# Attention and gated-delta stage of a hybrid trunk: a scaling removed, and 52 PSUM copies moved from VectorE to ScalarE

## The chip, the core and the metric

The kernel runs on one core of a Trainium2 chip. The metric is device time in microseconds (us), median of several executions. Engines are named as in the profile: PE (TensorE), DVE (VectorE), ACT (ScalarE), POOL (GpSimd), and SP, whose queue starts most DMAs.

## The reference, cut to what matters

One step of a two-layer trunk over 128 context and 512 latent tokens, width 1024. The first layer runs two mixers beside each other on one input projection:

```
s = einsum('bqhgd,bkhd->bhgqk', q_blk, k) * hd ** -0.5        # hd = 64, so the factor is 1/8
p = softmax(s, axis=-1)
out = einsum('bhgqk,bkhd->bqhgd', p, v)                       # 8 query heads, 2 key heads
...
def step(s, inp):                                             # gated delta rule, 4 heads, 2 directions
    v_new = u_c - w_c @ s
    o_c = qd_c @ s + qk_c @ v_new
    s = s * dec_c + kd_c^T v_new
```

An output projection, an MLP, then a Mamba-2 (SSD) layer with its own MLP follow. Softmax gives the same numbers if the scores are computed as s' = -s, and exp(min(s') - s') stands for exp(s - max(s)).

## The kernel before, in words

Matrix products are float32, often as high and low halves. `even` runs the first layer; the part that matters here begins when the input projections end (229 us in the profiled execution) and ends when the output projection's first product, `rps` on line 328, starts (507.95 us). In it two strands share all engines:

- `attention`, a generator, runs 4 blocks (2 key heads by 2 pairs of query heads). A block turns its queries (`stacks`: `qtps`, copied by ACT into `qs`, line 1238), then for each of 4 latent query tiles and 2 heads does `scores` into `scps` (line 1243: 4 matmuls, 512 and 256 keys) and `softmax`: a maximum over 768 keys on DVE (line 1249, `amx`), a scaling of it by -1/8 on DVE (line 1250), the exponential on ACT with that as bias (line 1252), a reciprocal on DVE (line 1253), a scaling on ACT (line 1255). The weights `p` are turned on PE four blocks at a time (`ptps`, line 1294) and copied out of PSUM into `pp` and `ppr` (line 1297), by DVE and ACT in turn. At a block's end 12 products `avps` (line 1303) make the output. There is one buffer of `scps`, so the next scores wait for the exponential.
- `delta_head` runs once for each of 4 heads, on two sets of buffers, so that heads go in pairs. It inverts a triangular matrix (products on lines 1032 and 1038 with DVE work between), then scans 4 chunks in both directions. One step of the scan makes `v_new` in a PSUM bank `pv` (lines 1094, 1095), scales it into `vk` on DVE (line 1098), copies it into `vn` on DVE (line 1100), multiplies `vk` into the other columns of the same bank (line 1102), from which DVE makes the next state `s` (line 1104); `vn` goes into the output `ops` (line 1107). The context chunk has its own copies of these lines (1120, 1122, 1124, 1130). A head ends with a norm and five turns (line 1146).

The code's order is one head, nine pieces of attention, then the other heads. The list that each engine gets is made at build time by a scheduler that plays the program in simulated time, and which may move an instruction ahead of independent ones. So a change of an operation's engine also changes the order around it, the order in later stages included. Each engine then runs its own list strictly in order.

The weights of the output projection (`wraw`, line 264) land in the two buffers that attention uses for `pp` (`ring`), so their load waits for the last `avps` that reads them. The residual `x` (2.5 MB, line 788) is loaded into the space of the delta heads' buffers, from ACT's queue.

Of the kernel before, what the change touches and what calls it, by code (L numbers as in the profile page):

```python
# [14 lines left out]
AF = mybir.ActivationFunctionType  # L15
ALU = mybir.AluOpType
AX = mybir.AxisListType
# [3 lines left out]
P = 128  # L21
# [181 lines left out]
class Prog:  # L203
# [713 lines left out]
    def delta_head(self, dn, pd, h, st_, gt):  # L917
        nc, v, g = self.nc, self.nc.vector, self.nc.gpsimd
# [5 lines left out]
        quad = lambda ap: ap.rearrange("p (a b) -> p a b", b=P)  # L924
# [9 lines left out]
        for ts_, ids in lots:  # L934
            pt = bank()
# [153 lines left out]
        for n in range(4):  # L1089
            for d in range(2):  # L1090
                c = n if d == 0 else 3 - n
                t = c + 1
                pv = bank()
                nc.tensor.matmul(pv[:, 0:P], X[:, 1 - d, t, :], values(d, t), start=True, stop=False)
                nc.tensor.matmul(pv[:, 0:P], wn[d][:, t, :], st[d], start=False, stop=True)
                if n < 3:
                    vk = dn.tile([P, P], F32, name="vk", tag=f"vk{d}")
                    v.tensor_scalar(out=vk, in0=pv[:, 0:P], scalar1=gt["ek"][:, d, t, h:h + 1], scalar2=None, op0=ALU.mult)
                vn = dn.tile([P, P], F32, name="vn", tag=f"vn{d}", bufs=2)
                v.tensor_copy(vn, pv[:, 0:P])  # L1100
                if n < 3:
                    nc.tensor.matmul(pv[:, P:2 * P], kk[:, t, :], vk, start=True, stop=True)
                    s = dn.tile([P, P], F32, name="s", tag=f"s{d}", bufs=2)
                    v.scalar_tensor_tensor(out=s, in0=st[d], scalar=dec[d][:, c:c + 1], in1=pv[:, P:2 * P], op0=ALU.mult, op1=ALU.add)
                po = self.pout.tile([P, 512], F32, name="ops", tag="o")
                nc.tensor.matmul(po[:, 0:P], qd[d][:, c, :], st[d], start=True, stop=False)
                nc.tensor.matmul(po[:, 0:P], qk[d][:, t, :], vn, start=False, stop=True)
                if n < 3:
                    st[d] = s
                if n < 2:  # L1110
                    nc.scalar.activation(out=o[:, t, :], in_=po[:, 0:P], func=AF.Copy, scale=rq[:, t:t + 1])
                else:
                    v.scalar_tensor_tensor(out=o[:, t, :], in0=po[:, 0:P], scalar=rq[:, t:t + 1], in1=o[:, t, :], op0=ALU.mult, op1=ALU.add)

        vns = []
        for d in range(2):
            pv = bank()
            nc.tensor.matmul(pv[:, 0:P], X[:, 1 - d, 0, :], values(d, 0), start=True, stop=True)
            vk = dn.tile([P, P], F32, name="vk", tag=f"vk{d}")
            v.tensor_scalar(out=vk, in0=pv[:, 0:P], scalar1=gt["ek"][:, d, 0, h:h + 1], scalar2=None, op0=ALU.mult)  # L1120
            vn = dn.tile([P, P], F32, name="vn0", tag=f"vn{d}", bufs=2)
            v.tensor_copy(vn, pv[:, 0:P])
            vns.append(vn)
            nc.tensor.matmul(pv[:, P:2 * P], kk[:, 0, :], vk, start=True, stop=True)
            s = dn.tile([P, P], F32, name="s0", tag=f"s{d}", bufs=2)
            nc.scalar.copy(out=s, in_=pv[:, P:2 * P])
            nc.sync.dma_start(out=self.io["o_sd"][d, h], in_=s)
# [14 lines left out]
        for ts_, c, cu in (((0,), CTX_P, CTX_U), ((1, 2, 3, 4), LAT_P, LAT_U)):  # L1142
            pt = bank()
# [67 lines left out]
    def attention(self, at, psc, pacc, qkv, keys, ota):  # L1211
# [10 lines left out]
        def stacks(kv, pr):  # L1222

            c0 = 272 + kv * 256 + pr * 128
            x = qkv[:, :, c0:c0 + 128].rearrange("p t (h e) -> p t h e", e=64)
            qs = at.tile([P, 2, NTOK], F32R, name="qs", tag="qs", bufs=2)
            for ts_ in ((0, 1), (2, 3), (4,)):
                n = len(ts_)
                y = x[:, ts_[0]:ts_[0] + n]
                hl = at.tile([P, 768], F32, name="p", tag="p", bufs=3)[:, :n * 256].bitcast(F32R).rearrange("p (t h a b) -> p t h a b", h=2, a=2, b=64)  # L1230
                nc.scalar.copy(out=hl[:, :, :, 0], in_=y)
                v.tensor_tensor(out=hl[:, :, :, 1], in0=y, in1=hl[:, :, :, 0].bitcast(F32), op=ALU.subtract)
                hf = hl.bitcast(F32).rearrange("p t h a b -> p t h (a b)")
                pt = bank("qtps")
                for j, t in enumerate(ts_):
                    for i in range(2):
                        nc.tensor.transpose(pt[:, (i * n + j) * P:(i * n + j + 1) * P], hf[:, j, i], self.ident)
                nc.scalar.copy(out=qs[:, :, ts_[0] * P:(ts_[0] + n) * P], in_=pt[:, :2 * n * P].rearrange("p (i c) -> p i c", i=2))
            return qs

        def scores(out, qs, kv, i, t, k0, k1):
# [3 lines left out]
        def softmax(sc, p):  # L1245

            n = sc.shape[1]
            mx, sm = (at.tile([P, 2], F32, name=m, tag=m, bufs=3)[:, :n] for m in ("amx", "asm"))
            v.tensor_reduce(out=mx, in_=sc, axis=AX.X, op=ALU.max)
            v.tensor_scalar(out=mx, in0=mx, scalar1=-scale, scalar2=None, op0=ALU.mult)  # L1250
            for i in range(n):
                nc.scalar.activation(out=p[:, i], in_=sc[:, i], func=AF.Exp, scale=scale, bias=mx[:, i:i + 1], accum_out=sm[:, i:i + 1])
            v.reciprocal(out=sm, in_=sm)
            for i in range(n):
                nc.scalar.activation(out=p[:, i], in_=p[:, i], func=AF.Copy, scale=sm[:, i:i + 1])
# [5 lines left out]
        for kv in range(2):  # L1261
            for pr in range(2):
                o = ota[kv * 2 + pr]
                qs = stacks(kv, pr)
                yield

                sc = psc.tile([P, 2 * 512], F32, name="scps", tag="sc")
                for i in range(2):
                    scores(sc[:, i * P:(i + 1) * P], qs, kv, i, 0, 0, P)
                pc = at.tile([P, 2, P], F32, name="pc", tag="pc")  # L1270
                softmax(quad(sc[:, :2 * P]), pc)
                yield
                pt = bank("ptps")
                for i in range(2):
                    nc.tensor.transpose(pt[:, i * P:(i + 1) * P], pc[:, i], self.ident)
                pct = at.tile([P, 2, P], F32, name="pct", tag="pct")
                v.tensor_copy(pct, quad(pt[:, :2 * P]))
                yield

                for t in range(1, NT):  # L1280
                    cols = slice((t - 1) * P, t * P)
                    ps = []
                    for i in range(2):
                        sc = psc.tile([P, 2 * 512], F32, name="scps", tag="sc")
                        scores(sc[:, 0:512], qs, kv, i, t, P, P + 512)
                        scores(sc[:, 512:768], qs, kv, i, t, P + 512, P + 768)
                        ps.append(at.tile([P, 768], F32, name="p", tag="p", bufs=3))
                        softmax(sc[:, :768].rearrange("p (o k) -> p o k", o=1), ps[i].rearrange("p (o k) -> p o k", o=1))
                        yield
                    for j in range(3):  # L1290
                        pt = bank("ptps")
                        for n in range(4):
                            x = ps[j][:, n * P:(n + 1) * P] if j < 2 else ps[n // 2][:, (4 + n % 2) * P:(5 + n % 2) * P]
                            nc.tensor.transpose(pt[:, n * P:(n + 1) * P], x, self.ident)  # L1294
                        dst = ring[j][:, :, cols] if j < 2 else rest.rearrange("p i c q -> p (i c) q")[:, :, cols]
                        turn += 1
                        (v.tensor_copy if turn % 2 else nc.scalar.copy)(out=dst, in_=quad(pt))
                    yield
                acc = bank("avps")
                for c in range(6):  # L1300
                    for i in range(2):
                        x = ring[i][:, c] if c < 4 else rest[:, i, c - 4]
                        nc.tensor.matmul(acc[rows[i]], val(1 + c, kv), x, start=c == 0, stop=c == 5)  # L1303
                nc.scalar.copy(out=o[:, LAT_U], in_=acc)
                acc = bank("avps")
                for i in range(2):
                    nc.tensor.matmul(acc[rows[i], :P], val(0, kv), pct[:, i], start=True, stop=True)
                v.tensor_copy(o[:, CTX_U], acc[:, :P])
                yield
# [435 lines left out]
```

## Time and profile before

| | us |
|---|---|
| median of 3 runs (2148.13 to 2157.08) | 2155.83 |
| the profiled execution, device time | 2143.07 |
| its span, first to last instruction | 2141.2 |
| PE busy in the span | 2029.4 |
| DVE busy | 1376.8 |
| ACT busy | 935.4 |

The profiled execution took 1.87 us more than its span, and 12.76 us less than the median of the runs. A busy PE is a PE with matmuls in it, not one at its peak: the same four score matmuls count 0.95 us at the full granted clock and 1.65 us at half of it.

### The profile page before, as it was taken

How to read it: one execution, taken by the hardware profiler on the slowest of the kernel's cores; microseconds unless marked ns; L12 is line 12 of the kernel's file. 1: busy time of each engine (PE TensorE's matmuls, PEld its weight loads, DVE VectorE, ACT ScalarE, POOL GpSimd, SP SyncE). 2: the span in 40 equal slices, each digit the busy share in tenths (PEclk: the TensorE clock that was granted, in tenths of full speed). 3: DMA queues.
4: the chain of work that ended last, by engine and by line, in shares of the span. 5: the costliest groups of instructions: out<-in, count | busy, mean ns of one | idle time of the engine just before them, and what ended most of it. 6: DMA issues, size and time to landing. Idle time of an engine off the chain costs nothing.

```text
span 2141.2 us, 32845 instructions
## 1 busy us (share of the span) xinstructions
PE 2029.4 (95%) x13227; PEld 1827.7 (85%) x13227; DVE 1376.8 (64%) x2628; ACT 935.4 (44%) x1959; POOL 147.3 (7%) x106
## 2 busy tenths in 40 slices
PE   6999698898899999999899999999999899999998
PEld 4989686775797989898799999999888888989896
DVE  6386777874886767664678886787634634343445
ACT  4344457573342423233259866666531332323131
POOL 1031302100000000000000001111110000000000
PEclk9999789898999999999999999999999999999999
DMA  7261101005255343332234343333341221212121
GB/s 328 85 241 40 38 1 35 1 12 198 100 188 190 134 148 136 141 124 95 89 101 148 129 146 120 114 133 126 117 159 67 91 97 60 79 60 99 59 79 50
DMA packets 55834, 233.31 MB, mean 109 GB/s; under 512 B 6074, under 2 KB 21186, under 8 KB 33922
## 3 DMA queue, kind: packets, MB, share of 16 engines
q1 hardware_dynamic: 45952, 216.63, 28.4%
q10 hardware_dynamic: 9730, 14.58, 1.9%
q8 instruction: 104, 1.70, 0.3%
q14 instruction: 48, 0.39, 0.1%
HBM read 222.76 MB, written 8.43 MB: 108 GB/s over the span
## 4 chain that ended last, share of the span: by engine, by line
PE 85%; DVE 9%; DMA 2%; ACT 2%; issue 1%; POOL 0%; ACTq 0%; SPq 0%; DVEq 0%; POOLq 0%
PE gps L300 41%; PE rps L328 28%; PE yps L1648 2%; PE atps L750 2%; PE offps L1662 1%; PE scps L1243 1%; PE dps L1032 1%; DMA X<-growd 1%; PE stps L1679 1%; DMA wraw<-wall 1%; PE avps L1303 1%; PE dps L1038 1%; PE ptps L1294 1%; DVE wlo L275 1%; PE xkps L1498 1%
## 5 line engine op out<-in xcount | busy, mean ns | idle before, releaser
L300 PE MATMUL gps<-hh,whi 128*128 128x322 f32 (+3 forms) x1552 | 488.6, 316 | 1.4 <-ACT hh L412 1.4
L300 PE MATMUL gps<-hh,wlo 128*128 128x322 f32 (+3 forms) x1552 | 486.5, 314 | 0.0
L300 PE MATMUL gps<-hl,whi 128*128 128x322 f32 (+3 forms) x1552 | 485.6, 313 | 0.0
L300 PEld LDWEIGHTS gps<-hh,whi 128*128 128x128 f32 (+1 forms) x1552 | 292.3, 189 | 7.9 <-issue 5.1
L300 PEld LDWEIGHTS gps<-hl,whi 128*128 128x128 f32 (+1 forms) x1552 | 292.4, 188 | 3.2 <-issue 2.8
L300 PEld LDWEIGHTS gps<-hh,wlo 128*128 128x128 f32 (+1 forms) x1552 | 292.4, 188 | 2.1 <-issue 1.7
L328 PE MATMUL rps<-wlo,hidh 128*128 128x512 f32 x640 | 253.3, 396 | 0.0
L328 PE MATMUL rps<-whi,hidh 128*128 128x512 f32 x640 | 252.3, 396 | 0.0
L328 PE MATMUL rps<-whi,hidl 128*128 128x512 f32 x640 | 250.5, 395 | 0.0
L272 ACT CAST whi<-wraw 128x1024 fp32r<-128x1024 f32 (+2 forms) x132 | 140.3, 1065 | 247.1 <-PE rps L328 176.3
L284 DVE TENSOR_TENSOR wlo<-wraw,whi 128x1024 fp32r<-128x1024 f32 x88 | 107.4, 1225 | 191.5 <-ACT whi L283 191.5
L300 PE MATMUL gps<-yh,whi 128*128 128x320 f32 x1024 | 227.1, 311 | 0.2 <-ACT yh L412 0.2
L275 DVE TENSOR_TENSOR wlo<-wraw,whi 128x1024 fp32r<-128x1024 f32 (+3 forms) x123 | 157.8, 1283 | 100.7 <-ACT whi L272 100.3
L283 ACT CAST whi<-wraw 128x1024 fp32r<-128x1024 f32 x88 | 91.8, 1049 | 269.6 <-PE rps L328 188.5
L300 PEld LDWEIGHTS gps<-yh,whi 128*128 128x128 f32 x1024 | 172.6, 189 | 1.0 <-ACT yh L412 0.7
L300 PE MATMUL gps<-yh,wlo 128*128 128x320 f32 x512 | 158.6, 310 | 0.0
L328 PEld LDWEIGHTS rps<-whi,hidh 128*128 128x128 f32 x640 | 120.3, 188 | 29.3 <-issue 1.2
L328 PEld LDWEIGHTS rps<-wlo,hidh 128*128 128x128 f32 x640 | 120.3, 188 | 28.8 <-issue 0.6
L328 PEld LDWEIGHTS rps<-whi,hidl 128*128 128x128 f32 x640 | 120.3, 188 | 28.6
L485 DVE SCALAR_TENSOR_TENSOR macc<-wraw,condst,macc 128x512 f32<-128x512 f32 x196 | 137.2, 752 | 5.6 <-ACT macc L488 5.6
L650 DVE TENSOR_SCALAR hr<-gps 128x320 f32<-128x320 f32 x128 | 62.9, 492 | 105.7 <-PE gps L300 105.6
L651 ACT ACTIVATE hr<-hr 128x320 f32<-128x320 f32 x128 | 60.2, 470 | 150.8 <-DVE hr L650 149.3
(412 smaller groups left out, 3509.7 us busy)
## 6 DMA issues: line engine op xcount, KB each, us to landing
wraw<-wall SPq DMA_DIRECT2D x158, 1024.0 KB
bc<-afs SPq DMA_DIRECT2D x40, 512.0 KB
Q<-afr SPq DMA_DIRECT2D x64, 128.0 KB
xt<-xt ACTq DMA_DIRECT2D x1, 2560.0 KB
X<-growd SPq DMA_DIRECT2D x8, 320.0 KB
x<-x ACTq DMA_DIRECT2D x1, 2560.0 KB
xd<-x ACTq DMA_DIRECT2D x1, 2560.0 KB
x<-xd SPq DMA_DIRECT2D x1, 2560.0 KB
```

The costliest lines, as they stand in the source:

```text
L272: self.nc.scalar.copy(out=hi, in_=raw[:, :, c:c + m])
L275: eng.tensor_tensor(out=lo, in0=raw[:, :, c:c + m], in1=hi.bitcast(F32), op=ALU.subtract)
L283: self.nc.scalar.copy(out=hi, in_=x)
L284: self.nc.vector.tensor_tensor(out=lo, in0=x, in1=hi.bitcast(F32), op=ALU.subtract)
L300: self.nc.tensor.matmul(ps, ws[k // KT][q // 2][:, k % KT, :], xs[q % 2][k][:, c], start=k == 0 and q == 0, stop=k == n - 1 and q == 2)
L328: nc.tensor.matmul(ps, parts[x][k][:, c], w[y][:, j, :], start=k == 0 and q == 0, stop=k == n - 1 and q == 2)
L485: nc.vector.scalar_tensor_tensor(out=a, in0=x, scalar=w, in1=a, op0=ALU.mult, op1=ALU.add)
L650: nc.vector.tensor_scalar(out=r, in0=ps, scalar1=0.0, scalar2=None, op0=ALU.max)
L651: nc.scalar.activation(out=r, in_=r, func=AF.Square)
L750: nc.tensor.matmul(ps[:, :n], x[k][:, TOFF[t]:TOFF[t] + P], w[:, k, :], start=k == 0 and q == 0, stop=k == KT - 1 and q == 2)
L1032: nc.tensor.matmul(py[:, t * 32:(t + 1) * 32], m32[:, t, :], mixed(Xc, t, l), start=True, stop=True)
L1648: nc.tensor.matmul(py[q * 64:q * 64 + 64, pr * P:(pr + 1) * P], X[t](1 + d)[:, hh * 64:hh * 64 + 64], D[t][:, d, hh, :], start=d == 0, sto ...
```

## The change

Four edits. (1) The queries' halves leave PSUM multiplied by -1/8 (on ACT, where they were copied before), so the scores come out negated and scaled; the softmax takes their minimum, which is the exponential's bias as it is, and the DVE scaling on line 1250 (36 of them) is gone. (2) The copy `vn` in the scan is made by ACT (32 instructions). (3) So is `vn` of the context chunk (8). (4) Of the 48 copies of turned weights ACT now makes 36 and DVE 12, where it was 24 and 24.

```
                 vn = dn.tile([P, P], F32, name="vn", tag=f"vn{d}", bufs=2)
-                v.tensor_copy(vn, pv[:, 0:P])
+                nc.scalar.copy(out=vn, in_=pv[:, 0:P])
...
             vn = dn.tile([P, P], F32, name="vn0", tag=f"vn{d}", bufs=2)
-            v.tensor_copy(vn, pv[:, 0:P])
+            nc.scalar.copy(out=vn, in_=pv[:, 0:P])
...
-                nc.scalar.copy(out=qs[:, :, ts_[0] * P:(ts_[0] + n) * P], in_=pt[:, :2 * n * P].rearrange("p (i c) -> p i c", i=2))
+                nc.scalar.activation(out=qs[:, :, ts_[0] * P:(ts_[0] + n) * P], func=AF.Copy, scale=-scale, in_=pt[:, :2 * n * P].rearrange("p (i c) -> p i c", i=2))
...
-            v.tensor_reduce(out=mx, in_=sc, axis=AX.X, op=ALU.max)
-            v.tensor_scalar(out=mx, in0=mx, scalar1=-scale, scalar2=None, op0=ALU.mult)
+            v.tensor_reduce(out=mx, in_=sc, axis=AX.X, op=ALU.min)
             for i in range(n):
-                nc.scalar.activation(out=p[:, i], in_=sc[:, i], func=AF.Exp, scale=scale, bias=mx[:, i:i + 1], accum_out=sm[:, i:i + 1])
+                nc.scalar.activation(out=p[:, i], in_=sc[:, i], func=AF.Exp, scale=-1.0, bias=mx[:, i:i + 1], accum_out=sm[:, i:i + 1])
...
-                        (v.tensor_copy if turn % 2 else nc.scalar.copy)(out=dst, in_=quad(pt))
+                        (nc.scalar.copy if turn % 4 else v.tensor_copy)(out=dst, in_=quad(pt))
```

From line 1250 on, line numbers of the changed kernel are lower by one. PE's list at the end of the stage, before: the last scores, the last turns, the last head's five turns, attention's output products, then the output projection.

```order
L1106 MATMUL ops<-s,qd_4983 128x128
L1107 MATMUL ops<-vn,dt 128x128
L1146 MATMUL dps<-con,M 128x128 x5
...
L1294 MATMUL ptps<-con,p 128x128 x4
L1146 MATMUL dps<-con,M 128x128 x5
L1294 MATMUL ptps<-con,p 128x128 x8
L1303 MATMUL avps<-pp,qkv 64x512 x8
L1303 MATMUL avps<-ppr,vc 64x512 x4
L1307 MATMUL avps<-pct,qkv 64x128 x2
L328 MATMUL rps<-whi,op 128x512 x5
```

And now, from the last turns on:

```order
L1293 MATMUL ptps<-con,p 128x128 x4
L1106 MATMUL ops<-s,qd_4947 128x128
L1107 MATMUL ops<-vn,dt 128x128
L1118 MATMUL dps<-vb,X 128x128 x2
L1302 MATMUL avps<-pp,qkv 64x512 x8
L1302 MATMUL avps<-ppr,vc 64x512 x4
L1106 MATMUL ops<-s,qd_4946 128x128
L1107 MATMUL ops<-vn,de 128x128
...
L1130 MATMUL dps<-vn_5239,de 128x128
L1130 MATMUL dps<-vn_5251,dt 128x128
L328 MATMUL rps<-whi,op 128x512 x5
```

Before, all products of the scan (lines 1094 to 1130) stood ahead of the last two score groups; now attention's output products stand among the last products of the scan, and one head's five turns have gone behind the first 64 products of the output projection.

PE's list in the first pair's scan, with what each waits for (the name of an engine stands for its semaphore), before:

```order
L1102 MATMUL dps<-vk,dk_957 128x128 [waits DVE_49]
L1107 MATMUL ops<-vn,de 128x128 [waits Pool_49]
L1102 MATMUL dps<-vk,dk_957 128x128 [waits DVE_49]
L1094 MATMUL dps<-vb,X 128x128 [waits DVE_49,Activation_49]
L1095 MATMUL dps<-s,Xt 128x128
```

and now:

```order
L1102 MATMUL dps<-vk,dk_957 128x128 [waits Activation_49]
L1107 MATMUL ops<-vn,de 128x128 [waits Pool_49]
L1102 MATMUL dps<-vk,dk_957 128x128 [waits Activation_49]
L1094 MATMUL dps<-vb,X 128x128 [waits DVE_49]
L1095 MATMUL dps<-s,Xt 128x128
```

The state's product on line 1102, which reads `vk`, waited for DVE; it now waits for ACT, which makes `vn` out of the same bank.

ACT's list at that place, now:

```order
L1251 ACTIVATE p,asm<-scps,amx 128x768 [waits DVE_49]
L1296 COPY pp<-ptps 128x4x128 [waits PE_49]
L1000 ACTIVATE vb<-dv_958,beta 128x128 [waits PE_49] x2
L1100 COPY vn<-dps 128x128 [waits DVE_49] x2
L1254 ACTIVATE p<-p,asm 128x768 [waits DVE_49]
L1296 COPY ppr<-ptps 128x4x128 [waits PE_49]
L1251 ACTIVATE p,asm<-scps,amx 128x768 [waits DVE_49]
L1111 ACTIVATE M<-ops,rq_960 128x128 [waits PE_49]
L1000 ACTIVATE vb<-dv_958,beta 128x128 [waits PE_49,Activation_49] x2
L1100 COPY vn<-dps 128x128 [waits DVE_49] x2
```

The two `vn` of a step (one for each direction) have come in between the exponential and the scaling of a softmax, and wait for DVE's `vk`.

ACT's list at the end of the stage, now:

```order
L1122 COPY vn_5251<-dps 128x128 [waits DVE_49,Activation_49]
L1303 COPY ota_979<-avps 128x512 [waits PE_49]
L1126 COPY s_5242<-dps 128x128 [waits DMAHW7_49,PE_49]
L1126 COPY s_5254<-dps 128x128 [waits DMAHW0_49,PE_49]
L788 DMA x<-x 128x5120 [waits DMAHW3_49,DMAHW4_49,DMAHW2_49,PE_49]
L283 CAST whi<-wraw 128x1024 [waits DMAHW5_49]
```

The load of `x` stood well ahead of attention's last exponentials; it now stands behind the last attention output, right ahead of the first split of the output projection's weights.

## Rows read from the trace of the kernel before

**Rows 1.** The page: engines over the span.
```profile
PE 2029.4 (95%) x13227; PEld 1827.7 (85%) x13227; DVE 1376.8 (64%) x2628; ACT 935.4 (44%) x1959; POOL 147.3 (7%) x106
```
**Rows 2.** Windows: from:to, length, busy PE PEld DVE ACT POOL, clock, DMA.
```profile
234.00:258.00 24.00, 13.35 (x61) 11.22 (x62) 23.43 (x56) 13.19 (x40) 12.91 (x10) 0.64 0.12 33
314.00:341.00 27.00, 26.42 (x232) 24.69 (x231) 20.94 (x73) 20.88 (x53) 0.00 (x0) 1.00 0.06 16
362.00:386.00 24.00, 16.41 (x93) 10.68 (x93) 22.24 (x46) 12.42 (x35) 16.79 (x12) 0.90 0.06 16
420.00:479.20 59.20, 55.55 (x470) 48.41 (x469) 44.93 (x158) 44.16 (x114) 0.00 (x0) 1.00 0.02 6
479.20:508.00 28.80, 17.52 (x72) 9.48 (x69) 13.01 (x40) 12.93 (x29) 0.00 (x0) 0.75 0.49 182
500.00:2141.00 1641.00, 1596.64 (x9734) 1439.02 (x9730) 1031.05 (x1725) 675.42 (x1306) 60.88 (x41) 0.99 0.33 115
```
**Rows 3.** Chain that ended last, the stage's end: start, length, what.
```profile
490.54 0.99 ACT p L1252 x2
...
496.26 5.79 PE avps L1303 x16
502.06 4.77 DMA wraw<-wall
...
506.85 1.05 ACT whi L283
...
507.95 7.15 PE rps L328 x24
```
**Rows 4.** PE in order of time, 366 to 508 us: start, length, instructions, idle before.
```profile
367.38 3.66 PE L1303 MATMUL avps<-pp,qkv 128*64 128x512 f32 x16
370.87 1.88 PE L1303 MATMUL avps<-ppr,vc 128*64 128x512 f32 x8
...
477.82 0.94 PE L1243 MATMUL scps<-kst,qs 128*128 128x512 f32 x4
...
478.82 0.39 PE L1107 MATMUL ops<-vn,dt 128*128 128x128 f32 x2
...
479.59 0.60 PE L1294 MATMUL ptps<-con,p 128*128 128x128 f32 x4
...
496.26 5.76 PE L1303 MATMUL avps<-pp,qkv 128*64 128x512 f32 x16 [0.68 <-ACT ppr L1297]
```
**Rows 5.** Lines, 229 to 500 us: shapes, count, busy us, mean ns, idle before.
```profile
L1297 DVE COPY pp<-ptps 128x512 f32<-128x512 f32 x16 | 11.0, 687 | 1.2 <-PE ptps L1294 0.9
L1297 ACT COPY pp<-ptps 128x512 f32<-128x512 f32 x16 | 9.3, 582 | 11.0 <-PE ptps L1294 11.0
L1250 DVE TENSOR_SCALAR amx<-amx 128x1 f32<-128x1 f32 (+1 forms) x36 | 6.2, 173 | 0.3
```
**Rows 6.** Tile views: ns min/median/max of one, and waiters.
```profile
L1100 DVE COPY vn<-dps x32: 276/282/292, 314.7 to 473.7; 128x128 f32<-128x128 f32 x32
L1126 ACT COPY s<-dps x8: 247/262/276, 338.3 to 477.6; 128x128 f32<-128x128 f32 x8
L1255 ACT ACTIVATE p<-p,asm x32: 929/938/954, 242.9 to 492.0; 128x768 f32<-128x768 f32 x32
```
**Rows 7.** Waits, 229 to 500 us: us in total, times, longest.
```profile
ACT p L1252 <- DVE amx L1250: 13.8, 12, 3.7
PE scps L1243 <- ACT p L1252: 8.7, 7, 2.9
PEld dps L1102 <- DVE vn L1100: 1.4, 3, 0.6
```
**Rows 8.** DVE in order of time, around 245 us.
```profile
244.37 0.95 DVE L1249 TENSOR_REDUCE amx<-scps 128x1 f32<-128x768 f32 x1
...
246.64 0.15 DVE L1250 TENSOR_SCALAR amx<-amx 128x1 f32<-128x1 f32 x1
```
**Rows 9.** Windows while `x` lands.
```profile
482.00:486.00 4.00, 2.29 (x8) 1.65 (x8) 2.91 (x11) 2.79 (x8) 0.00 (x0) 0.69 0.96 410
```

## The prediction

> **What bounds the kernel now.** The page says PE is busy for 95% of the span and DVE for 64% [rows 1], so over the whole kernel nothing is to be had from DVE. The change touches one stage, from 229 us to the start of the output projection at 507.95 us, so I read that stage by windows [rows 2]; the reader should see three kinds of stretch. While a pair of heads scans (314 to 341, 420 to 479.2), PE is busy for 26.42 of 27 us and 55.55 of 59.2, at a granted clock of 1.00: PE is the bound there, DVE has a quarter of its time free. While a pair is prepared (234 to 258, 362 to 386), DVE is busy for 23.43 and 22.24 of 24 us, PE for 13.35 and 16.41, at a clock of 0.64 and 0.90: DVE is the bound. At the end (479.2 to 508) no engine is: PE 17.52 of 28.8 at a clock of 0.75, DVE 13.01, ACT 12.93.
>
> The end I read in the chain and on PE's own timeline. PE's last product of the scan starts at 478.82 us and takes 0.39 [rows 4]. What follows is attention alone, one engine after another: scores, DVE's maximum, ACT's exponential, turns, copies, the output products, and then 4.77 us for the first weights of the output projection, which land in attention's buffers, and 1.05 us for their split [rows 3]. So the stage ends with attention's strand, late by what that strand lost earlier. Where it lost time the waits tell: ACT waited 13.8 us for the scaling on line 1250, PE 8.7 us for the exponential [rows 7]. That scaling is short (0.173 us on the mean [rows 5]) but queues behind other DVE work: one maximum ends at 245.32 us and its scaling starts at 246.64 [rows 8].
>
> **The change, part by part.** All sums are against the profiled execution: 2143.07 us, a span of 2141.2 and 1.87 around it. The median of the runs, 2155.83, lies 12.76 higher; I take a difference worked out on the one for the other.
>
> DVE loses 36 scalings, 6.2 us; 40 `vn` copies of 0.282 us [rows 6], 11.3 us; and 12 copies of turned weights of 0.687 [rows 5], 8.2 us: 25.7 us in all. ACT gains 40 copies of 0.262 us (the row of line 1126 is the same shape from the same PSUM tiles [rows 6]), 10.5 us, and 12 of 0.582 [rows 5], 7.0 us: 17.5 us. The factor -1/8 rides on a copy that ACT made anyway, the minimum replaces a maximum of the same shape: both nothing, either way.
>
> *The end of the stage.* Attention's strand gets shorter by the wait for the scaling, and the built order has moved accordingly: its output products stand among the last products of the scan. So the 28.7 us between the end of the scan (479.21) and the first output product (507.95) go. What PE did in them must still be done, ahead of the scan's end, at full clock: six groups of turns at 0.60, two score groups at 0.94, and 24 output products at 3.66 + 1.88 [rows 4], 11.0 us. And the weights' load and split stay: 5.9 us from the last `avps` that reads the buffer (502.02) to the first product. PE's list has 1.88 us of `avps` and eight scan products, at 0.39 at most 3.1 us, in that time; about 1 us stays open. Term: -28.7 + 11.0 + 1 = **-16.7 us**. The head's five turns that went behind the first 64 products hide there: at the 7.15 us for 24 of the chain's last row [rows 3], 64 take 19 us, and the head's norm is needed only for products behind them.
>
> *The stretches where DVE is the bound.* No `vn` falls there. Of the scalings and weight copies (14.4 us over 279 us of stage) a share of 48/279 would be 2.5 us. Bounds: 0, and 5 if PE's lower clock comes back with it. I take **-2**.
>
> *`vn` on ACT.* 24 state products on line 1102 and 8 on line 1124 now wait for ACT, whose list holds exponentials and scalings of 0.94 us [rows 6]. Queued behind a stalled state product is PE's whole list, and then DVE's `s`. Below, this costs nothing: before, the same products waited for the copy on DVE, 1.4 us in three waits by the weight loads [rows 7]. Above, all 32 wait for a full 0.94: 30 us. ACT is busy 75% of the long scan stretch (44.16 of 59.2); half a length at that share is 0.35 us, 11 us over 32, if nothing lay between `vk` and its product on PE's list. There the scheduler has put turns or scores mostly. I take a quarter: **+3**.
>
> On the row, the product that writes the other half of the bank waited for a copy that it does not read (line 1102 for `vn`, 1.4 us [rows 7]). The Trainium skill has a rule for this: "PSUM — Partial Sum Buffer", section "PSUM bank collisions raise a hardware error", says that two engines may not touch one bank of the same partitions at once, two reads included, and are to be guarded by bank. By it `vk` on DVE and `vn` on ACT cannot lie beside each other, and moving the copy to a second engine shortens no step of the scan; the waits in the built order agree. A sum that let ACT copy while DVE scales would be lower by 32 copies of 0.28, 9 us; I don't take it.
>
> *The load of `x`.* It landed during the end of the stage at 410 GB/s [rows 9], with nothing waiting. Now its 2560 KB (2.62 million bytes) start beside the weights' load, on which PE waits. Bounds: 0, since the weights are asked for first, and 6.4 us (all of it at 410). I take **+1.5**.
>
> *Later stages.* The order in the SSD layer moved too, with no operation changed. PE is busy there for 1596.64 of 1641 us [rows 2]; I take nothing, and 3 us either way.
>
> Sum: -16.7 - 2 + 3 + 1.5 = -14.2. The profiled execution would take 2129, the median **2142 us**.
>
> **The rivals.** (a) *The scan hangs on ACT.* Each state product finds ACT inside an exponential or a scaling. With a mean wait w in place of my 0.09 us the sum is -17.2 + 32w: even at w = 0.54, slower by 0.5% at 0.87, and at 0.94 it is +13, 2169 us. For it: PE's list is strict, and the two `vn` of a step stand right behind an exponential. Against: PE's products between, and that the old wait was 1.4 us in all. (b) *The end changes its owner.* Attention is used up earlier, so the last steps of the scan lie bare: behind the last scores PE's list has three steps of one head, each at least three products of 0.39, a copy on ACT of 0.26 and two DVE operations like `vn` of 0.28, about 2 us plus hand-overs, with little to put between. Two of them bare and the same once more at the pair's end are 8 to 10 us; the sum is -5, 2151 us. For it: before, attention's products filled PE in the scan. Against: four groups of turns and the output products still stand among these steps. (c) *More is won.* With attention pulled ahead into the stretches where PE ran at 0.64 and 0.90, the clock there is 1.00: 13.35 us times 0.36 and 16.41 times 0.10 are 6.4 us; with the full 5 for DVE the sum is near -24, 2132 us. Against: POOL and the loads of `X` hold these stretches too.
>
> **How the numbers follow.** A measurement of this kernel tells a difference of about 0.5%, 10.8 us, from none. Chances: my forecast 0.45 (2136 to 2150), (b) 0.27, (a) 0.14, (c) 0.14. Faster by over 0.5% is below 2145: most of mine, all of (c), little of (b): 0.53. Slower is above 2166.6: most of (a): 0.12. The rest is 0.35. The range takes in (c), with the SSD layer's 3 us and the unknown load, and reaches into (a): 2122 to 2163, with some 0.15 left out, mostly above.
>
> **What would show it.** The changed profile should show the first output product 12 to 20 us earlier (near 492), attention's `avps` at full clock beside the scan's last products, no idle of several us on PE just ahead of them, DVE's busy time lower by about 26 us and ACT's higher by about 17. Waits of PE's line 1102 for ACT's `vn` of more than 10 us in all would show (a); PE idle between scan products after the last scores, (b); an unchanged clock in the preparation of both pairs speaks against (c); the first weights landing later than 4.77 us shows the load of `x`. I am wrong if the stage's end stays where it is, or if the time moves behind it.

## The result, and the profile after

The changed kernel took 2128.03 us (median of 6 executions, 2126.35 to 2136.43) against 2154.57 for the kernel before (6 executions, 2148.13 to 2157.08): a ratio on record of 0.9896, 95% interval 0.9872 to 0.9921 (it is not the quotient of the two medians, 0.9877). Both kernels run again gave 2130.05 and 2149.5, 0.9904 (0.9872 to 0.9936). So 19 to 27 us were won by the medians, 21 to 22 by the ratios. I had forecast 2142, from 2122 to 2163, with a chance of 0.53 for faster; the time lies in that range, but below the 2136 to 2150 of my own sum.

The page of the changed kernel, engines over the span, answers [rows 1]. DVE's busy time fell by 22.4 us, ACT's rose by 7.1. The 52 copies that ACT took over have 18.2 us by their lines, about what I had summed; the page's busy time rises less, since ACT's instructions overlap (its lines add up to over 1030 us in a busy time of 942.5):

```profile
span 2134.3 us, 32795 instructions
...
PE 2032.8 (95%) x13227; PEld 1835.8 (86%) x13227; DVE 1354.4 (63%) x2540; ACT 942.5 (44%) x2011; POOL 141.8 (7%) x106
```

The windows of the changed kernel, in the columns of [rows 2], with 262 to 300 us beside them; 479.20 to 500.00 ends at the new end of the stage:

```profile
234.00:258.00 24.00, 15.12 (x76) 12.87 (x76) 22.61 (x52) 15.81 (x44) 12.52 (x10) 0.78 0.12 34
262.00:300.00 38.00, 34.19 (x173) 29.40 (x174) 24.02 (x50) 17.18 (x35) 7.71 (x6) 0.65 0.00 1
...
362.00:386.00 24.00, 19.12 (x134) 17.84 (x134) 18.62 (x56) 16.31 (x47) 9.04 (x8) 0.86 0.13 39
420.00:479.20 59.20, 57.56 (x451) 51.45 (x452) 35.83 (x104) 37.60 (x98) 0.00 (x0) 0.90 0.01 2
479.20:500.00 20.80, 18.27 (x124) 12.88 (x122) 11.45 (x42) 12.85 (x42) 0.00 (x0) 1.00 0.24 88
500.00:2134.00 1634.00, 1592.47 (x9719) 1438.35 (x9719) 1034.26 (x1746) 674.43 (x1317) 55.76 (x41) 0.99 0.33 116
```

In both preparations PE does more than before and DVE less. The end is no longer half empty: PE is busy for 18.27 of 20.8 us at a clock of 1.00, where it was 17.52 of 28.8 at 0.75. In the long scan stretch, though, the clock is 0.90 where it was 1.00 (0.92 and 0.97 in the second profiles of the two kernels), and from 262 to 300 us it is 0.65 in both profiles of the changed kernel, where the kernel before has 0.78 and 0.86.

The chain that ended last, at the stage's end (start, length, what), answers [rows 3]:

```profile
490.48 3.59 PE avps L1302 x16
...
494.13 4.67 DMA wraw<-wall
...
498.82 1.05 ACT whi L283
...
499.92 15.16 PE rps L328 x64
```

PE in order of time at the same place (start, length, instructions, idle before and its releaser), for [rows 4]:

```profile
479.99 0.95 PE L1243 MATMUL scps<-kst,qs 128*128 128x512 f32 x4
...
490.41 3.65 PE L1302 MATMUL avps<-pp,qkv 128*64 128x512 f32 x16
...
498.49 0.39 PE L1130 MATMUL dps<-vn,dt 128*128 128x128 f32 x2
499.92 1.43 PE L328 MATMUL rps<-whi,op 128*128 128x512 f32 x5 [1.05 <-ACT whi L283]
```

The reader is to see that the two strands now end together. `avps` runs at full clock (3.65 us), the scan's last product ends at 498.88, behind it, and the output projection begins 1.04 us later, where there were 28.7 us between them. But the scan ends 19.7 us later than before (479.21, now 498.88), and so the first output product came only 8.0 us earlier. The second pair of profiles has the scan's end at 480.89 and 495.60 and the first output product at 509.66 and 496.73, 12.9 us apart.

The waits in the stage (us in total, times, longest), for [rows 7]:

```profile
PEld scps L1243 <- ACT p L1251: 7.6, 6, 2.3
...
PE scps L1243 <- ACT p L1251: 6.4, 6, 2.0
...
ACT p L1251 <- DVE amx L1249: 5.3, 7, 1.7
DVE s L1104 <- PE dps L1102: 3.8, 3, 2.3
...
PEld dps L1102 <- ACT vn L1100: 0.5, 2, 0.3
```

ACT's wait for the bias fell from 13.8 us to 5.3. PE's state product waits for ACT's `vn` no longer than it did for DVE's (0.5 us, 1.4 before). DVE, which makes the next state from that product, does wait longer for it: 3.8 us in three waits, where it waited once, for 0.5 us, before.

### The profile page after: what moved, and what is told of

It is laid out like the page before. It is cut to its first block, busy times and chain, and to the rows that moved or that the text cites. A ratio compares the mean times of both kernels' runs of the same rounds, so it can differ in the third digit from the quotient of the medians.

```text
span 2134.3 us, 32795 instructions
## 1 busy us (share of the span) xinstructions
PE 2032.8 (95%) x13227; PEld 1835.8 (86%) x13227; DVE 1354.4 (63%) x2540; ACT 942.5 (44%) x2011; POOL 141.8 (7%) x106
## 4 chain that ended last, share of the span: by engine, by line
PE 88%; DVE 7%; DMA 2%; ACT 2%; issue 1%; SPq 0%; DVEq 0%; ACTq 0%
PE gps L300 42%; PE rps L328 28%; PE yps L1647 2%; PE atps L750 2%; PE offps L1661 1%; PE dps L1038 1%; PE dps L1032 1%; DMA wraw<-wall 1%; PE scps L1243 1%; PE stps L1678 1%; DMA X<-growd 1%; PE ptps L1293 1%; PE avps L1302 1%; PE xkps L1497 1%; PE modps L459 1%
## 5 line engine op out<-in xcount | busy, mean ns | idle before, releaser
L328 PEld LDWEIGHTS rps<-wlo,hidh 128*128 128x128 f32 x640 | 120.3, 188 | 28.8 <-issue 0.6
```

What stands on the lines that cost most here:

```text
L328: nc.tensor.matmul(ps, parts[x][k][:, c], w[y][:, j, :], start=k == 0 and q == 0, stop=k == n - 1 and q == 2)
```

## The experiments

Theories: that of the strand (attention's chain hangs behind the scan at the stage's end; the change shortens the chain, and once both strands end together no more is to be had) and that of the load (what counts is VectorE's time, about 0.8 us for each us that it loses). Two more came in: the granted clock, and the order (any edit shuffles the built lists, and that alone may move the time). A table first. The time is the median, with the number of executions, and each ratio is to executions of the kernel before that ran beside it. The rest is from each kernel's one profile: the stage from 229 us to the first output product; its end, which is the part of it behind the scan's last product; PE and DVE busy in the stage; and PE's idle time, the length less PE's busy time.

| kernel | us (n) | ratio to before, 95% | stage | end | PE busy | PE idle | DVE busy |
|---|---|---|---|---|---|---|---|
| before | 2154.57 (6) | | 278.95 | 28.7 | 230.50 | 48.45 | 207.81 |
| changed | 2128.03 (6) | 0.9896, 0.9872 to 0.9921 | 270.92 | 1.0 | 233.37 | 37.55 | 180.81 |
| before again | 2148.16 (10) | 0.9987, 0.9968 to 1.0005 | 280.66 | 28.8 | 230.82 | 49.84 | 207.25 |
| changed again | 2130.05 (4) | 0.9904, 0.9872 to 0.9936 | 267.73 | 1.1 | 230.65 | 37.08 | 180.98 |
| edit 1 alone | 2132.35 (5) | 0.9905, 0.9871 to 0.9939 | 257.93 | 0 | 224.50 | 33.43 | 197.38 |
| edit 1, second time | 2133.21 (6) | 0.9910, 0.9886 to 0.9934 | 258.68 | 0 | 224.69 | 33.99 | 197.53 |
| edits 2, 3 | 2134.18 (4) | 0.993, 0.991 to 0.995 | 268.61 | 19.6 | 221.75 | 46.86 | 200.25 |
| edit 4 | 2145.61 (10) | 0.9982, 0.9964 to 1.0 | 281.32 | 22.5 | 234.98 | 46.34 | 195.99 |
| edits 1, 4 | 2134.59 (4) | 0.9927, 0.9907 to 0.9947 | 266.69 | 14.4 | 224.01 | 42.68 | 194.40 |
| edits 1, 2, 3 | 2135.22 (6) | 0.9926, 0.9896 to 0.9955 | 266.88 | 0 | 228.46 | 38.42 | 190.28 |
| before, turns swapped | 2152.18 (10) | 1.0007, 0.9986 to 1.0028 | 286.81 | 21.4 | 243.51 | 43.30 | 205.37 |
| changed, spare scalings | 2131.96 (4) | 0.9915, 0.9892 to 0.9937 | 267.87 | 1.5 | 231.19 | 36.68 | 185.46 |
| edits 2, 3, spare work | 2155.55 (12) | 1.0018, 1.0005 to 1.0031 | 288.03 | 20.6 | 242.69 | 45.34 | 212.85 |
| changed, all 48 on ACT | 2116.74 (5) | 0.9841, 0.9817 to 0.9864 | 251.46 | 0.2 | 220.57 | 30.89 | 171.05 |

PE has nearly the same products in the stage in every row (1576 to 1593 in the profiles), so its busy time differs mostly by the granted clock. From the first output product to the end of the span the profiles have 1633 to 1639 us, whichever kernel: to within 6 us, what is won or lost lies in this stage.

The end is the strand's own part. It is all but gone (1.5 us at most) in the rows with edit 1, except edits 1 and 4, where attention's output products and the weights' load are left behind the scan; the other edited rows have one score group behind it in place of two, and 19.6 to 22.5 us. The end alone does not make the time. The scan's last product ends at 479.2 and 480.9 us in the kernel before and at 478.1 with edits 2 and 3, but at 487.8 with edit 4, 494.5 with the turns swapped and 496.4 with the spare work: there the end's gain is lost ahead of it. One profile of a kernel is little; the mean granted clock is known of every execution. Its median is 0.965 to 0.966 for the kernel before and 0.966 with edit 4, 0.962 with the turns swapped, 0.963 with the spare work on DVE for the scan copies, 0.968 to 0.974 in the faster kernels, and 0.975 with all 48 copies on ACT.

**Both kernels again.** No edit.

> The kernel before, unchanged, for a second profile and for the clock of each run. Strand theory (the gain is the end of the stage, where attention's strand hung behind the scan) and load theory (the gain is 25.7 us less work on DVE) both expect 0 against before, within 0.4%. Clock theory (a good part of the 26 us between the medians is the granted clock inside the stage, which differs between executions) expects runs of 2143 to 2157 whose spans go with the clock: one hundredth of mean clock in 2150 us is 43 us at half clock in place of 21.5 at full, so 21.5 us; the first profile had 0.968 at 2141, so runs near 2155 should show about 0.962.

> The changed kernel, unchanged, for a second profile. All theories expect -1.0% (near 2128). Clock theory: the first profile (2134.3 span, clock 0.967) was the slowest of six; a profile at 0.971 should have fewer slices at half clock between 262 and 300 and between 392 and 452 us, and the stage's end near 490 in place of 499.9.

The difference stands. The profiles of one kernel agree in PE's idle time to 1.4 us; idle fell by some 11 to 13 us through the change, and PE's busy time did not fall. The second profile of the changed kernel has a mean clock of 0.967 like the first, so what its executions at 0.971 do in the stage is not shown.

**Edit 1 alone**, the queries' factor and the minimum; `vn` and the turned weights' copies are those of the kernel before.

```
-            v.tensor_reduce(out=mx, in_=sc, axis=AX.X, op=ALU.max)
-            v.tensor_scalar(out=mx, in0=mx, scalar1=-scale, scalar2=None, op0=ALU.mult)
+            v.tensor_reduce(out=mx, in_=sc, axis=AX.X, op=ALU.min)
```

> The softmax edit alone (negated scores, minimum as bias); copies as before. By the built order the scan's last products stand behind the last scores, as in the changed kernel. Strand theory: most of the gain, -14 to -24 us, near 2135. Load theory: in proportion to DVE's 6.2 of 25.7 us, -6 us, near 2148. Order lottery (any change shuffles the lists and moves the time by 10 us or so): no sign given.

> Edit 1 alone a second time, beside the others. Theory of the strand with a cap: 2128 to 2135, the same as the whole change to within 3 us. Theory of the load (VectorE loses 6.2 us of 25.7): 5 us, 2145.

All but a few us of the change's gain, twice, for 6 of the 26 us that DVE loses. That speaks against the load and for the strand: attention's last `avps` starts at 466.8 us (496.3 before), and ACT's wait for the bias is 6.0 us (13.8 before). Here the scan is what ends last, and its last steps lie partly bare in the profile: from that `avps` on PE is idle for 2.9 of 20.2 us at a clock of 0.86. In the stage the state product waits longer than before (0.6 us) for the copy that is still DVE's:

```profile
PE dps L1102 <- DVE vn L1100: 3.4, 2, 2.8
```

**The turns of the weights' copies swapped** in the kernel before: the same 24 copies on each engine, beginning with the other one.

```
-                        (v.tensor_copy if turn % 2 else nc.scalar.copy)(out=dst, in_=quad(pt))
+                        (nc.scalar.copy if turn % 2 else v.tensor_copy)(out=dst, in_=quad(pt))
```

> The kernel before with DVE and ACT exchanged in the copies of turned weights, 24 and 24 still: the same work on each engine, another order. Its list has one score group less behind the scan than before. Strand theory: -2 to -5 us, one group of the end of the stage. Load theory: 0. Order lottery: a change of 8 us or more either way.

The time is that of the kernel before, to within the interval. But the same work in another order has 13 us more of PE busy time in its stage, at a lower clock, and 5 us less of idle. Windows of this kernel:

```profile
262.00:300.00 38.00, 35.70 (x178) 33.60 (x178) 27.86 (x58) 17.46 (x34) 5.69 (x5) 0.60 0.01 1
420.00:460.00 40.00, 39.89 (x254) 34.95 (x253) 22.38 (x63) 16.06 (x38) 0.00 (x0) 0.72 0.00 1
```

and of the kernel before:

```profile
262.00:300.00 38.00, 35.98 (x236) 33.72 (x237) 31.85 (x78) 19.23 (x39) 5.07 (x4) 0.78 0.01 1
420.00:460.00 40.00, 37.24 (x331) 31.75 (x330) 27.70 (x92) 27.47 (x70) 0.00 (x0) 1.00 0.01 1
```

PE is as busy in the one as in the other, and does 178 and 254 of its products where the kernel before does 236 and 331 (244 and 334 at 0.86 and 0.96 in its second profile). Products differ in size, so the counts are a rough measure. Idle time that an order saves can so come back as a lower clock.

**The scan copies alone** (edits 2 and 3).

> The two scan copies (vn, 40 of them) on ScalarE alone, softmax and weights as before. By the built order one score group and four groups of turns still stand behind the scan's last product (before: two and six). Strand theory: -5 to +3 us, the softmax strand keeps its scaling. Load theory: 11.3 of 25.7 us, so -11 us, near 2143. Rival (a) of the prediction, the scan hangs on ScalarE: slower by 5 us or more.

15 us, where the strand's theory had taken 5 at most and the load's 11. The profile shows where: the scan's last product ends 1 to 3 us earlier than before, and from there to the first output product are 19.6 us in place of 28.7. Lines of this kernel:

```profile
477.66 0.39 PE L1107 MATMUL ops<-vn,dt 128*128 128x128 f32 x2
...
497.61 2.48 PE L328 MATMUL rps<-whi,op 128*128 128x512 f32 x5 [3.66 <-ACT whi L283]
```

So most of the stage's 10 to 12 us are the strand's, by the one score group that no longer stands behind the scan, and by a clock of 0.91 there (0.75 before). PE's idle time is hardly lower (46.86), its busy time is 8.7 us less. From 262 to 300 us this kernel's clock is 0.86, which is no gain: the kernel before has 0.78 in one profile and 0.86 in the other.

**The weights' copies alone** (edit 4), and **edits 1 and 4**.

> The copies of turned weights 36 to ScalarE and 12 to VectorE alone. The list's end is as in e5. Strand theory: -5 to +2 us. Load theory: 8.2 of 25.7 us, so -8 us, near 2146.

> The changed kernel with the scan copies back on VectorE (softmax and weight edits). The list's end has no score behind the scan, but the 14 output products still stand behind it. Strand theory: near the changed kernel, -14 to -22 us, some 3 to 5 short of it for the output products. Load theory: 14.4 of 25.7 us, -13 us. If scan copies on ScalarE cost what I took (3 us), this is 3 us faster than the strand alone would be.

Edit 4 alone is worth 4 us, at the edge of what 10 executions tell; behind edit 1 it adds nothing. Edits 1 and 4 do not part the theories, which had both taken about the 15 us measured. The changed kernel is this one with the scan copies on ACT: 2134.59 us without them there, 2128.03 and 2130.05 with, and the intervals of the ratios overlap. So on ACT the copies cost nothing that these runs can tell.

**The changed kernel with spare scalings on DVE**: 36 scalings like those that the change removed, into a tile that nothing reads. Nothing is left out of the computation.

```
             v.tensor_reduce(out=mx, in_=sc, axis=AX.X, op=ALU.min)
+            md = at.tile([P, 2], F32, name="amd", tag="amd", bufs=3)[:, :n]
+            v.tensor_scalar(out=md, in0=mx, scalar1=-scale, scalar2=None, op0=ALU.mult)
```

> The changed kernel with the 36 scalings put back on VectorE into a tile that nothing reads, so that VectorE has its 6.2 us again but no exponential waits for them. Strand theory: as the changed kernel within 4 us. Load theory: 6 us slower than it, near 2134.

They kept their place behind the minimum, 7.5 us of DVE in all, and cost 2 to 4 us against the two sets of the changed kernel, inside the interval. Lines of this kernel (instructions, count, busy us, mean ns, idle before):

```profile
L1251 DVE TENSOR_SCALAR amd<-amx 128x1 f32<-128x1 f32 x32 | 4.7, 146 | 0.3
...
L1251 DVE TENSOR_SCALAR amd<-amx 128x2 f32<-128x2 f32 x4 | 2.8, 697 | 0.1
```

So the scaling's time on DVE costs little off the strand. That fits edit 1 having taken away its place between the maximum and the exponential. The proof is not complete: edit 1 also has another built order, and no run takes the wait away and keeps the order.

**The scan copies on ACT, and spare work on DVE for them.**

```
+                vd = dn.tile([P, 64], F32, name="vd", tag="vd", bufs=1)
+                v.tensor_scalar(out=vd, in0=kk[:, t, 0:64], scalar1=gt["ek"][:, d, t, h:h + 1], scalar2=None, op0=ALU.mult)
+                v.tensor_scalar(out=vd, in0=kk[:, t, 64:128], scalar1=gt["ek"][:, d, t, h:h + 1], scalar2=None, op0=ALU.mult)
```

> The copies vn on ScalarE alone (edits 2 and 3), and VectorE gets its load back off the strand: for each of the 40 copies two scalings of 128x64, from SBUF, into a tile that nothing reads. So VectorE's work stays about that of the kernel before, and only the step of the scan (and the order that follows from it) changes. Theory of the strand (what counts is that attention no longer hangs behind the scan at the end): the gain of the copies alone, 15 us, stays to within 4 us: 2131 to 2140, the last output block of attention starting near 487 us as it does with the copies moved alone. Theory of the load (the gain is VectorE's time, 0.78 us for each us that it loses): the gain goes, 2146 to 2152, and that block starts near 497.

The whole gain of edits 2 and 3 is gone and 5 us more, as the load's theory said, and worse. The end is about as long as with the copies alone (20.6 us, 19.6); the loss lies ahead of it. But the test was not the one that I meant. The spare scalings depend on nothing in the scan, and the scheduler moved them ahead: by the tile's view the last of them starts at 311 us. Lines of this kernel, 226 to 520 us:

```profile
L1103 DVE TENSOR_SCALAR vd<-dk,ek 128x64 f32<-128x64 f32 x32 | 14.2, 466 | 0.2
...
L1102 DVE TENSOR_SCALAR vd<-dk,ek 128x64 f32<-128x64 f32 x32 | 13.9, 441 | 2.3 <-PE gps L300 2.2
...
L1128 DVE TENSOR_SCALAR vd<-dk,ek 128x64 f32<-128x64 f32 x8 | 2.0, 246 | 0.1
...
L1127 DVE TENSOR_SCALAR vd<-dk,ek 128x64 f32<-128x64 f32 x8 | 1.9, 243 | 0.1
```

That is 32.0 us of DVE put into the preparation of the first pair, where DVE is the bound: the window 229 to 311 of this kernel,

```profile
229.00:311.00 82.00, 65.26 (x314) 58.14 (x316) 72.10 (x219) 36.70 (x89) 21.16 (x16) 0.63 0.09 22
```

and of edits 2 and 3 without it:

```profile
229.00:311.00 82.00, 63.84 (x422) 55.83 (x423) 62.87 (x156) 42.40 (x101) 20.30 (x16) 0.81 0.06 18
```

PE is busy for as long, but gets through 314 products in place of 422, at 0.63 in place of 0.81. Attention's first `avps` starts 12 us later (307.65, 295.80). Of the 19.4 us that the stage is longer, PE's busy time has 20.9 and its idle time -1.5. In this kernel, then, DVE's time in a preparation counts, and its price is paid in PE's clock. Whether the scan copies' shorter place in the strand is worth anything by itself, this run does not say.

**Edits 1 to 3.**

> Edits 1 to 3, the turned weights' copies left as they were. VectorE loses 17.5 us. If each edit's gain were its own, those of the softmax (17 to 20 us) and of the scan copies (15) would add: 2115 to 2118. Theory of the strand with a cap (both edits free the same wait at the stage's end, after which the two strands end together and nothing is left to free): 2128 to 2135. Theory of the load: 0.78 of 17.5, 14 us, 2136.

15 us: the edits do not add, as a cap has it. The load's theory had taken 2136, so the time alone does not part them, and the six executions spread over 16 us (2129.75 to 2146.01). In the profile attention is done early (last `avps` at 473.3) and the scan is not (its last product ends at 496.0).

**All 48 copies of turned weights on ACT.**

```
-                        (nc.scalar.copy if turn % 4 else v.tensor_copy)(out=dst, in_=quad(pt))
+                        nc.scalar.copy(out=dst, in_=quad(pt))
```

> The changed kernel with all 48 copies of turned weights on ScalarE; VectorE loses 12 more of 0.687 us, 8.2 us. Theory of the load: 0.78 of it more than the change, 6 us: 2124. Theory of the strand with a cap: no more than the change, 2127 to 2134. If ScalarE becomes what the strand waits for (its copies queue behind exponentials and scalings of 0.94 us), some us slower than the change: 2135 to 2142, with waits of VectorE and TensorE for ScalarE's pp of several us more.

The fastest of all, 2116.74 us, 0.9841 (0.9817 to 0.9864) of the kernel before and 11 to 13 us faster than the change; none of the three expectations had it. Against the cap: it has both more idle time taken out (30.89) and more of the clock. ACT did not become the bound (its copy waits for the turns 7.8 us in all, 14.8 in the changed kernel). Windows of this kernel, 8 us each:

```profile
261.00:269.00 8.00, 7.41 (x55) 6.58 (x54) 6.44 (x14) 7.36 (x14) 5.04 (x4) 0.96 0.00 0
269.00:277.00 8.00, 7.16 (x60) 6.63 (x59) 7.70 (x21) 6.17 (x16) 2.82 (x2) 1.00 0.02 4
277.00:285.00 8.00, 8.00 (x64) 6.25 (x64) 6.00 (x14) 5.18 (x12) 0.00 (x0) 1.00 0.00 0
285.00:293.00 8.00, 8.00 (x61) 5.75 (x58) 3.26 (x8) 0.65 (x2) 0.00 (x0) 1.00 0.01 2
293.00:301.00 8.00, 8.00 (x90) 7.64 (x89) 5.90 (x23) 6.02 (x18) 0.00 (x0) 1.00 0.00 0
```

and of the changed kernel:

```profile
261.00:269.00 8.00, 8.00 (x39) 7.62 (x38) 5.38 (x11) 5.48 (x10) 5.34 (x4) 0.53 0.00 0
269.00:277.00 8.00, 6.72 (x51) 5.83 (x50) 7.76 (x17) 4.42 (x12) 1.22 (x1) 1.00 0.01 2
277.00:285.00 8.00, 5.48 (x27) 5.48 (x27) 5.50 (x12) 4.11 (x7) 1.42 (x2) 0.61 0.01 2
285.00:293.00 8.00, 8.00 (x40) 8.00 (x40) 3.46 (x8) 1.10 (x3) 0.00 (x0) 0.50 0.00 0
293.00:301.00 8.00, 8.00 (x29) 3.66 (x30) 2.92 (x7) 2.38 (x7) 0.00 (x0) 0.61 0.00 0
```

The two part at 261 us. Up to there, from 229 us, PE has done as much in the one as in the other (91 products here, 92 in the changed kernel), and behind it PE is busy or nearly so in both; but this kernel runs at 0.96 and the changed one at 0.53. What brought the clock back earlier the runs do not show. Then, at 277 us, PE of the changed kernel waits 2.55 us for DVE's `Xt` (line 1034), the clock falls, and PE works without any gap from 285 to 301 us at 0.50 and 0.61. In the other it has no such gap, stays at 1.00, and starts the first `avps` at 282.25 us where the changed kernel does at 294.70. The 16 products of that `avps` take 3.65 us there and 5.86 in the changed kernel. The changed kernel's second profile has the same clocks in these windows (0.53, 1.00, 0.61, 0.50, 0.61). These 12.5 us are near the difference of the medians, though the stages of the profiles differ by 16 to 19 us. Whether the earlier clock, one of the twelve moved copies or the order that came with them makes the difference, the runs do not tell apart.

## Why the prediction was right, and where it was off

**Direction and place: right.** All of the gain lies ahead of the first output product, edit 1 alone brings most of it, which with the spare scalings speaks for the scaling's place on the strand, and later stages gave nothing: 0 with 3 us either way was taken, and 1633 to 1636 us measured in the four profiles of the two kernels. The number is in part luck: the median fell below the 2136 to 2150 that I had given my own sum, while the profiled execution, for which the sum was made, took 2136.43 in place of 2129, and 2133.03 the second time.

**The end of the stage (-16.7): the mechanism held, the size was short of it in the profile.** The stretch behind the scan went from 28.7 us to 1.0 (28.8 to 1.1 in the second pair of profiles), as the term says. But it let the scan's end move by 11.0 us, the work done ahead "at full clock", and it moved by 19.7 (14.7 in the second pair). The step that failed is the full clock: from 420 to 479.2 us it was 0.90, from 262 to 300 us 0.65. An estimate of the price, PE's busy time times what the clock lacks to 1.00, summed over windows of 2 us from 229 to 479.2 us: 25.9 and 28.5 us in the profiles of the kernel before, 38.4 and 35.7 in those of the changed one. That is 7 to 12 us more, enough for what the scan's end moved beyond the term (8.7 and 3.7 us). The whole stage is 8.0 and 12.9 us shorter, where my terms for it came to 14.2.

**The preparations (-2): the right sign, but too simple a measure.** PE does more in the same 24 us (15.12 and 19.12 busy). What the clock does in and behind them can weigh more than either bound of 0 and 5, as the spare work of 32 us shows (20.9 us of PE busy time).

**`vn` on ACT (+3): nothing that the runs can tell.** 0.5 us of PE's waits, and edits 1 and 4 without these copies are no faster than the changed kernel; rival (a), the scan hanging on ACT, is refuted with it. A step of the changed kernel on DVE, ACT and PE (start, length) shows the order in one bank:

```profile
454.78 0.57 DVE L1098 TENSOR_SCALAR vk<-dps,ek 128x128 f32<-128x128 f32 x2
...
457.23 0.27 ACT L1100 COPY vn<-dps 128x128 f32<-128x128 f32 x1
...
457.87 0.28 ACT L1100 COPY vn<-dps 128x128 f32<-128x128 f32 x1
...
458.49 0.39 PE L1102 MATMUL dps<-vk,dk 128*128 128x128 f32 x2
```

ACT's copies start behind both of DVE's scalings, the first 1.9 us behind them, and the product behind the copies. The Trainium skill's rule ("PSUM — Partial Sum Buffer", section "PSUM bank collisions raise a hardware error") would have it so, and the rows agree in the order; whether the two would lie beside each other without it, no run here shows. In this step ACT was at other work until its copies, an exponential among it, and PE filled the time with ten products of an inversion (line 1025, from 457.30 us): so a copy that comes late cost PE little.

**The load of `x` (+1.5): nothing.** It is issued at 497.45 us, and the first weights landed in 4.67 us (4.77 before).

**Rival (b)**, the bare end of the scan, is not in the changed kernel: PE is idle for 2.5 of the last 20.8 us. Edit 1 alone has a little of it (2.9 us), and it did not keep that kernel from being nearly as fast. **Rival (c)**, more won through the clock, is nearest to the time (2132) but not by its own sign: in the preparation of the first pair the clock rose from 0.64 to 0.78, in that of the second it fell from 0.90 to 0.86; in the second pair of profiles it stayed at 0.71 in the first and fell from 0.92 to 0.86 in the second.

**From one execution to the median.** The largest part of the miss (2142 for 2128) is the step "I take a difference worked out on the one for the other". The profiled executions differ by 6.6 us (2143.07 to 2136.43), 14.6 in the second pair; the medians by 19 to 27. The executions of one kernel run at different mean clocks, and their times go with it: the kernel before has 2139.3 us of span at 0.973 and 2158.5 at 0.961, the changed kernel 2134.3 at 0.967 and 2126.3 at 0.972. At 0.967 the kernel before has 2146.2 to 2149.5, the changed one 2130.9 to 2134.3: 12 to 19 us, about what I had forecast. The rest goes with the clock, 0.965 to 0.966 in the median of the kernel before, 0.970 to 0.971 of the changed one. In which part of the span the unprofiled executions got it stays open, since only one execution of each run has a trace.

**The theories.** That of the strand explains edit 1, the copies alone (by the shorter end) and why the edits do not add, but its cap fell with the 48 copies. That of the load explains neither edit 1 nor the 36 spare scalings; it comes near in the time of edits 1 to 3 and of 1 and 4, and it holds for work that falls into a preparation. What is left is a sum: the stage is PE's busy time at the clock granted, plus its idle time, and an edit can take from the one and give to the other. That another order of the same work can move the clock's part is seen in the swapped turns: 13 us of PE busy time in one profile, and a mean clock of 0.962 against 0.966 in the median of all executions. How to choose an order for it is not shown, and since every edit here also changed the order, no run parts the two fully.

## What to carry to other kernels

Ask of a small operation where it stands, not how long it takes: 6 us of scalings between a reduction and an exponential were worth 17 us in this kernel, and nearly the same operations off that strand cost 2 to 4. Where two strands share a stage, gains of edits need not add: here 17 and 15 us made 15 together. And when a scheduler makes the order, spare work put in for a test may be moved to where it hurts: look up where it ran before reading its time.

## What the runs showed of the hardware

At half clock PE can be fully busy and stay there for many us: 8.00 of 8.00 us busy at 0.50 in the changed kernel from 285 to 293 us, behind a stretch with 5.48 of 8 us busy. The 16 products of one `avps` took 5.86 us from 294.70 in that kernel, at 0.61 from 293 to 301, and 3.65 in the kernel with all 48 copies on ACT, at 1.00. The mean clock of a whole execution of one kernel varied from 0.961 to 0.973, and its span with it by 19 us. The spare scalings of 128x64 took 0.24 us on the mean on lines 1127 and 1128 and 0.44 to 0.47 on lines 1102 and 1103, up to 2.18, the same operation in the same 85 us; the cause stays open.
